# A decoder layer on one core: the down projection's products S4·R22 and S3·T3 one behind the other, T4 made a stage earlier, L22 and S3 kept divided

## The chip, the core and the metric

The kernel runs on one core of a Trainium2 chip. The metric is the device time of one execution in microseconds (us); the median of several runs counts. The engines are TensorE (PE in the rows; PEld is its weight load), VectorE (DVE), ScalarE (ACT), GpSimd (POOL) and SyncE (SP). SP and POOL issue transfers between DRAM and the on-chip memory; the rows write their queues as SPq and POOLq.

## The reference

One decoder layer over 1024 tokens of width 1024, in float32. The part that the change touches is the channel-mixing sub-layer at its end:

```
u = x * (1.0 + scale2) + shift2
h = jnp.square(jax.nn.relu(u @ w_up[l] + b_up[l]))        # 1024 x 4096
y = h @ w_down[l] + b_down[l]                             # 1024 x 1024
x = _layer_norm(DEEPNORM_ALPHA * x + (1.0 + gate2) * y, ln2_g[l], ln2_b[l])
```

Ahead of it stand the token-mixing sub-layer (a gated recurrence and a retention branch, merged by gates, and an output projection with a layer norm of its own) and the modulation vectors.

## The kernel before

**Precision.** Every float32 product is three fp32r products: `split` (L171 to L173) divides an operand into a high part (an ACT copy, L172) and a low part (a DVE subtraction, L173), and `mm3` (L177 to L179) adds high·high, high·low and low·high into one PSUM bank.

**Up projection.** `seven` makes the hidden rows in groups, each for 256 hidden rows j (16 of them) and all tokens, by seven products of quarter blocks; the first group is plain (`up_plain`). Its sums leave PSUM on DVE (L443). `use_square` applies the squared ReLU and makes, for each j, seven left operands of the down projection: L11, L12, L22 and the sums S1 to S4 of quarters of h (128 hidden rows by 512 tokens each). `keep_h` (L1488) writes each to DRAM (`h_d`, 256 KB) by POOL's queue.

**Down projection.** `down_seven` multiplies h by w_down, again with seven products of quarter blocks: left operands L and S by right operands R11, R21, R22 (quarters of w_down) and T1 to T4 (differences of them). Each product runs over 16 pairs j of hidden rows, 12 PE instructions (`multiply`) for a j, into four PSUM banks: set X (tags d, d, d, b) or set Y (a, a, c, c). The seven stand in four stages, and within a stage the two products alternate j by j:

```
stages = ((("L12", "R21", "Y", True), ("L11", "R11", "X", True)),
          (("S1", "T1", "Y", True), ("S2", "T2", "X", False)),
          (("S4", "R22", "Y", False), ("S3", "T3", "X", False)),
          (("L22", "T4", "X", False),))
```

For step n of this sequence `load(n)` brings the left operand from DRAM by SP's queue (tile hr, 4 buffers), and `prepare(n)` makes the right operand from the raw rows of w_down on DVE and splits both into one U tile (14 buffers of 8 KB, of which 4 hold T2 for all j). `prepare` runs five steps ahead of `multiply`, `load` three steps ahead of `prepare`. T4 = W21 - T2 is made in the third stage, over T2.

**Behind the products.** When a product's 16 pairs are done, its banks are copied (`keep`) or added (`add`, L1621) to the eight row blocks of the output in SBUF, row0 to row7, 128 tokens each. `first_part` (L1603, L1606, L1607: times the gate, plus the residual zp, statistics) runs on half a row block, `second_part` on a whole one: the aggregate (L1376), L1377, a power on POOL (L1378), then for each half L1613 and L1614 on DVE and the output transfer (L1615). Work put into the list `later` is taken one piece per step. In the last stage the last eight pairs (DOWN_TAIL) are multiplied row block by row block (tt = 0 to 3), each followed by its first and second part.

**What sets the order.** The order in which the code records the work, and a scheduler that interleaves it on each engine by when it could start; the order excerpts below are what it made.

Of the kernel before, what the change touches and what calls it, by code (L numbers as in the profile page):

```python
# [19 lines left out]
P = 128  # L20
# [23 lines left out]
DOWN_TAIL = 8  # L44
N_LARGE = 14

# [5 lines left out]

H_DEFER = 4


# [71 lines left out]
class Trunk:  # L127
# [1359 lines left out]
    def keep_h(self, j, name, t):  # L1487
        self.nc.gpsimd.dma_start(self.h_d[j][name], t)  # L1488

# [31 lines left out]
    def up_plain(self):  # L1521
        wt = [self.W(("up", 0, t)) for t in (0, 1)]
        places = iter("grrrgrg")
        tile = lambda: (self.tp.tile([P, 512], F32, tag="relu", bufs=4, name=self.uid("relu")) if next(places) == "r" else
                        self.wp.tile([P, 512], F32, tag="gate", bufs=2, name=self.uid("relu")))
        use = self.use_square(0, tile, (1, 1))
        for half in (0, 1):
            for m in (0, 1):
                use(m, half, self.dense_T(*wt[m], half), True)
                if (half, m) == (0, 0):  # L1530
                    yield


    def down_seven(self):
# [6 lines left out]
                  (("S1", "T1", "Y", True), ("S2", "T2", "X", False)),  # L1541
                  (("S4", "R22", "Y", False), ("S3", "T3", "X", False)),
                  (("L22", "T4", "X", False),))
        seq = [(s, j, p) for s, st in enumerate(stages) for j in range(J) for p in range(len(st))]
        t2 = [self.ut(F32) for _ in range(J // 4)]
        T2 = [t2[j // 4][:, j % 4] for j in range(J)]
        loaded, parts, raws = {}, {}, {}

        def load(n):
            s, j, p = seq[n]  # L1550
            t = loaded[n] = self.hp.tile([P, 512], F32, tag="hr", bufs=4, name=self.uid("hr"))
            nc.sync.dma_start(t, self.h_d[j][stages[s][p][0]])

        def prepare(n):
            s, j, p = seq[n]
            left, right = stages[s][p][:2]
            if n + 3 < len(seq) and n + 3 not in loaded:
                load(n + 3)
            if p == 0 and s < 3:
                raws[j] = self.W(("dn", s, j))  # L1560
            r = raws.get(j)
            tmp = lambda: self.hp.tile([P, 512], F32, tag="tf", bufs=2, name=self.uid("tf"))
            if right == "R21":
                src = r[0][:, 1]
            elif right == "R11":
                src = r[0][:, 0]
            elif right == "T1":
                src = self.t1 = tmp()
                V.tensor_tensor(src, r[0][:, 512:], r[0][:, :512], op=ALU.subtract)
            elif right == "T2":  # L1570
                src = T2[j]
                V.tensor_tensor(src, r[1], self.t1, op=ALU.subtract)
            elif right == "R22":
                src = r[0][:, 1]
            elif right == "T3":
                src = tmp()
                V.tensor_tensor(src, r[0][:, 1], r[0][:, 0], op=ALU.subtract)
                V.tensor_tensor(T2[j], r[1], T2[j], op=ALU.subtract)
            else:
                src = T2[j]  # L1580
            u = self.ut()
            self.split(u[:, 0], u[:, 1], loaded.pop(n))
            self.split(u[:, 2], u[:, 3], src)
            parts[n] = u

# [46 lines left out]
        for n, (s, j, p) in enumerate(seq):  # L1632
# [5 lines left out]
            if later:  # L1638
                later.pop(0)()
            if s == 3 and j >= J - DOWN_TAIL:  # L1640
                if j == J - 1:
# [9 lines left out]
            for tt in range(4):  # L1651
# [6 lines left out]
                elif (s, p) == (1, 0):  # L1658
                    keep(Y, 4 + tt, up)
                elif (s, p) == (1, 1):  # L1660
                    keep(X, tt, up)
                elif (s, p) == (2, 0):
                    add(Y, tt, up)
                    later.append(lambda tt=tt: first_part(tt, up))
                elif (s, p) == (2, 1):
                    add(X, 4 + tt, up)
                    later.append(lambda tt=tt: first_part(4 + tt, up))
            if (s, p) == (2, 1):
                later += [lambda tt=tt: second_part(tt) for tt in range(4)]


def build(ctx, tc, ins, out):
# [13 lines left out]
    k.ga_d, k.gb_d, k.y1_d = dt("ga_d", KT), dt("gb_d", KT), dt("y1_d", KT)  # L1686
    k.h_d = [{c: k.dp.tile([P, 512], F32, name=f"h_d{j}{c}") for c in ("L11", "L12", "L22", "S1", "S2", "S3", "S4")}
             for j in range(FT // 2)]
# [49 lines left out]
    two = lambda j, cs: wd[256 * j:256 * j + 256, cs].rearrange("(k p) c -> p k c", p=P)  # L1738
    for st in range(3):
        for j in range(FT // 2):  # L1740
            pcs = {0: [two(j, lo)],
                   1: [wd[256 * j:256 * j + P, :], wd[256 * j + P:256 * j + 256, up]],
                   2: [two(j, up), wd[256 * j + P:256 * j + 256, lo]]}[st]
            rest.append((pcs, [(("dn", st, j), "raw", None)]))
# [103 lines left out]
    with ExitStack() as sh:  # L1848
# [12 lines left out]
        with ExitStack() as se:  # L1861
            k.ev = k.pool("ev2", "left", se)
            k.e_bufs = 14
            up = k.seven(ups)
            next(up)
# [36 lines left out]
```

## Time and profile before

| | us |
|---|---|
| median of 3 runs | 2258.92 |
| lowest, highest run | 2257.53, 2260.2 |
| the profiled execution | 2258.29 |
| its span (first to last instruction) | 2256.5 |

The profiled execution lies 0.63 us below the median, and its span ends 1.79 us below its own time. The mean granted TensorE clock is 0.997 of full speed. The times in all rows are those of the profiled execution. A row's "idle before" is the time in which the engine stood still ahead of the instruction, and the name behind the arrow is what ended it.

### The profile page before, as it was taken

Reading aid. Unit: us, or ns where it says so; the run is one execution under the profiler, and the core shown is the slowest. Engines: PE = TensorE matmul, PEld = TensorE weight load, DVE = VectorE, ACT = ScalarE, POOL = GpSimd, SP = SyncE. Lnnn points to the kernel's source line nnn. Section 1 sums busy time; section 2 is a strip of 40 time slices with the busy share of each in tenths; the row PEclk is TensorE's granted clock in tenths of the full one; section 3 lists DMA queues with packets and bytes.
Section 4 is the critical chain, followed back from the end, with each engine's and each line's share of the span. In section 5 each row is a group of like instructions: output and inputs, shape, how many; then the busy total and the mean of one; then the engine's idle time right before and its main releaser. Section 6 shows DMA issues by size and latency. Waiting matters only on the chain. (4 is left out here: it accounts for less than half of the span.)

```text
span 2256.5 us, 29106 instructions
## 1 busy us (share of the span) xinstructions
PE 2215.7 (98%) x10214; PEld 1822.1 (81%) x10214; DVE 1660.4 (74%) x3024; ACT 967.3 (43%) x1625; POOL 282.1 (13%) x444
## 2 busy tenths in 40 slices
PE   6999999999999999999999999999999999999997
PEld 4888887888888888888877777888878888888886
DVE  7757777667878678889765556977796665577669
ACT  3533334433333333332354434443575555553441
POOL 0110111111111101010112221112112112100001
PEclk9999999999999999999999999999999999999999
DMA  9554644544343522113176667655344444787653
GB/s 309 183 167 161 208 136 164 169 135 140 135 141 117 172 89 75 57 66 104 60 254 201 209 204 258 211 163 179 112 150 156 152 154 151 265 289 247 215 164 131
DMA packets 229075, 375.33 MB, mean 166 GB/s; under 512 B 17096, under 2 KB 127424, under 8 KB 228672
## 3 DMA queue, kind: packets, MB, share of 16 engines
q1 hardware_dynamic: 200176, 279.66, 38.4%
q0 software_dynamic: 28432, 93.35, 11.2%
q8 instruction: 80, 1.31, 0.2%
q14 instruction: 67, 0.55, 0.1%
q10 hardware_dynamic: 320, 0.45, 0.1%
HBM read 275.87 MB, written 97.53 MB: 165 GB/s over the span
## 5 line engine op out<-in xcount | busy, mean ns | idle before, releaser
L177 PE MATMUL psd<-U,bh 128*128 128x512 f32 x616 | 241.9, 393 | 1.8 <-DVE e L443 1.8
L178 PE MATMUL psd<-U,bh 128*128 128x512 f32 x616 | 239.8, 389 | 0.0
L179 PE MATMUL psd<-U,bl 128*128 128x512 f32 x616 | 239.8, 389 | 0.0
L172 ACT ACTIVATE bh<-s 128x512 fp32r<-128x512 f32 x204 | 128.6, 631 | 239.7 <-PE psd L178 78.9
L178 PE MATMUL psd<-U,wh 128*128 128x512 f32 x504 | 199.6, 396 | 3.6 <-DVE U L173 3.3
L177 PE MATMUL psd<-U,wh 128*128 128x512 f32 x504 | 202.4, 405 | 0.4 <-ACT U L172 0.4
L179 PE MATMUL psd<-U,wl 128*128 128x512 f32 x504 | 201.8, 400 | 0.0
L172 ACT ACTIVATE bh<-raw 128x512 fp32r<-128x512 f32 x153 | 97.1, 638 | 206.1 <-PE psd L178 100.4
L173 DVE TENSOR_TENSOR bl<-raw,bh 128x512 fp32r<-128x512 f32 x153 | 104.5, 689 | 105.8 <-ACT bh L172 92.9
L173 DVE TENSOR_TENSOR bl<-s,bh 128x512 fp32r<-128x512 f32 x204 | 139.5, 685 | 49.4 <-ACT bh L172 49.3
L177 PEld LDWEIGHTS psd<-U,bh 128*128 128x128 f32 x616 | 115.6, 188 | 31.0 <-issue 3.5
L172 ACT ACTIVATE U<-hr 128x512 fp32r<-128x512 f32 x112 | 70.5, 630 | 151.0 <-issue 56.7
L179 PEld LDWEIGHTS psd<-U,bl 128*128 128x128 f32 x616 | 115.7, 188 | 24.2
L178 PEld LDWEIGHTS psd<-U,bh 128*128 128x128 f32 x616 | 115.7, 188 | 23.5
L172 ACT ACTIVATE wh<-raw 128x512 fp32r<-128x512 f32 (+1 forms) x78 | 52.7, 695 | 173.8 <-PE psd L178 136.2
L177 PE MATMUL psa<-U,bh 128*128 128x512 f32 x312 | 121.4, 389 | 0.0
L178 PE MATMUL psa<-U,bh 128*128 128x512 f32 x312 | 121.4, 389 | 0.0
L179 PE MATMUL psa<-U,bl 128*128 128x512 f32 x312 | 121.4, 389 | 0.0
L178 PEld LDWEIGHTS psd<-U,wh 128*128 128x128 f32 x504 | 95.5, 190 | 25.3 <-DVE U L173 7.3
L177 PEld LDWEIGHTS psd<-U,wh 128*128 128x128 f32 x504 | 95.1, 190 | 19.1 <-ACT U L172 2.3
L179 PEld LDWEIGHTS psd<-U,wl 128*128 128x128 f32 x504 | 95.3, 189 | 18.7
L173 DVE TENSOR_TENSOR U<-hr,U 128x512 fp32r<-128x512 f32 x112 | 76.7, 685 | 44.7 <-ACT U L172 44.5
(446 smaller groups left out, 5630.7 us busy)
## 6 DMA issues: line engine op xcount, KB each, us to landing
raw<-in_w_in SPq DMA_DIRECT2D x126, 512.0 KB
raw<-in_w_down SPq DMA_DIRECT2D x48, 512.0 KB
raw<-in_w_pb SPq DMA_DIRECT2D x36, 512.0 KB
adw<-in_w_ada SPq DMA_DIRECT2D x64, 256.0 KB
raw<-in_w_up SPq DMA_DIRECT2D x32, 512.0 KB
adw<-in_w_ada SPq DMA_DIRECT2D x16, 512.0 KB
rv_d<-e POOLq DMA_DIRECT2D x32, 256.0 KB, 3.8
rg_d<-e POOLq DMA_DIRECT2D x32, 256.0 KB, 2.4
```

Of the source, the lines that this page charges most:

```text
L172: pin(self.nc.scalar.activation(hi, src, AF.Copy))
L173: pin(self.nc.vector.tensor_tensor(lo, src, hi.bitcast(F32), op=ALU.subtract))
L177: r = mm(out, wh, uh, start=start, stop=False, skip_group_check=more)
L178: mm(out, wh, ul, start=False, stop=False, skip_group_check=more)
L179: return r, mm(out, wl, uh, start=False, stop=stop, skip_group_check=more)
```

## The change

The third stage becomes two: all 16 pairs of S4·R22 into Y, then all 16 of S3·T3 into X; L22·T4 follows as before. T4 is computed in the second stage behind the split of T2, from the lower rows of w_down that are there for T2; so the second stage loads these rows whole, and the new third stage loads the quarter W22 once more. The work of row blocks 0 to 3 is put into `later` behind S4·R22 and that of rows 4 to 7 behind S3·T3. L22 and S3 are split in the up projection, by `keep_h`, into two tiles (tag parts; 4 buffers for the first group, 3 for the others) and written as two fp32r tensors; the down projection loads the two straight into a U tile by POOL's queue, and takes that tile at `load`, not at `prepare`. U has 15 buffers instead of 14, and the program is built with a scratch of 4096 bytes for dynamic transfers where the default stood.

In the excerpts and the diff lines of the change stand two (helpers) or some twenty (`down_seven`) further down: L175 is L173, L399 is L397, L445 is L443, L1516, L1520, L1522, L1527 are L1506, L1510, L1512, L1517, L1594 is L1577, L1623, L1626, L1627, L1633, L1634, L1641 are L1603, L1606, L1607, L1613, L1614, L1621, and L1378, L1379 are L1376, L1377.

```diff
 DOWN_TAIL = 8
-N_LARGE = 14
+N_LARGE = 15
...
 H_DEFER = 4
+
+H_PARTS = ("L22", "S3")
...
     def keep_h(self, j, name, t):
-        self.nc.gpsimd.dma_start(self.h_d[j][name], t)
+
+        d = self.h_d[j][name]
+        if name not in H_PARTS:
+            self.nc.gpsimd.dma_start(d, t)
+            return
+        parts = [self.h_tile(F32R) for _ in d]
+        self.split(*parts, t)
+        for a, b in zip(d, parts):
+            self.nc.gpsimd.dma_start(a, b)
...
         stages = ((("L12", "R21", "Y", True), ("L11", "R11", "X", True)),
                   (("S1", "T1", "Y", True), ("S2", "T2", "X", False)),
-                  (("S4", "R22", "Y", False), ("S3", "T3", "X", False)),
-                  (("L22", "T4", "X", False),))
+                  (("S4", "R22", "Y", False),), (("S3", "T3", "X", False),), (("L22", "T4", "X", False),))
         seq = [(s, j, p) for s, st in enumerate(stages) for j in range(J) for p in range(len(st))]
+        last = len(stages) - 1
         t2 = [self.ut(F32) for _ in range(J // 4)]
         T2 = [t2[j // 4][:, j % 4] for j in range(J)]
         loaded, parts, raws = {}, {}, {}
 
         def load(n):
             s, j, p = seq[n]
+            d = self.h_d[j][stages[s][p][0]]
+            if isinstance(d, list):
+                u = loaded[n] = self.ut()
+                for e in (0, 1):
+                    nc.gpsimd.dma_start(u[:, e], d[e])
+                return
             t = loaded[n] = self.hp.tile([P, 512], F32, tag="hr", bufs=4, name=self.uid("hr"))
-            nc.sync.dma_start(t, self.h_d[j][stages[s][p][0]])
+            nc.sync.dma_start(t, d)
 
         def prepare(n):
             s, j, p = seq[n]
             left, right = stages[s][p][:2]
             if n + 3 < len(seq) and n + 3 not in loaded:
                 load(n + 3)
...
-            if p == 0 and s < 3:
+            if p == 0 and s < last:
...
             elif right == "T2":
                 src = T2[j]
-                V.tensor_tensor(src, r[1], self.t1, op=ALU.subtract)
+                V.tensor_tensor(src, r[1][:, 512:], self.t1, op=ALU.subtract)
             elif right == "R22":
-                src = r[0][:, 1]
+                src = r[0]
             elif right == "T3":
                 src = tmp()
                 V.tensor_tensor(src, r[0][:, 1], r[0][:, 0], op=ALU.subtract)
-                V.tensor_tensor(T2[j], r[1], T2[j], op=ALU.subtract)
             else:
                 src = T2[j]
-            u = self.ut()
-            self.split(u[:, 0], u[:, 1], loaded.pop(n))
+            u = loaded.pop(n)
+            if stages[s][p][0] not in H_PARTS:
+                hr, u = u, self.ut()
+                self.split(u[:, 0], u[:, 1], hr)
             self.split(u[:, 2], u[:, 3], src)
+            if right == "T2":
+                V.tensor_tensor(src, r[1][:, :512], src, op=ALU.subtract)
             parts[n] = u
...
-            if s == 3 and j >= J - DOWN_TAIL:
+            if s == last and j >= J - DOWN_TAIL:
...
                 elif (s, p) == (2, 0):
                     add(Y, tt, up)
                     later.append(lambda tt=tt: first_part(tt, up))
-                elif (s, p) == (2, 1):
+                elif (s, p) == (3, 0):
                     add(X, 4 + tt, up)
                     later.append(lambda tt=tt: first_part(4 + tt, up))
-            if (s, p) == (2, 1):
+            if (s, p) == (2, 0):
                 later += [lambda tt=tt: second_part(tt) for tt in range(4)]
...
-    k.h_d = [{c: k.dp.tile([P, 512], F32, name=f"h_d{j}{c}") for c in ("L11", "L12", "L22", "S1", "S2", "S3", "S4")}
+    k.h_d = [{c: [k.dp.tile([P, 512], F32R, name=f"h_d{j}{c}{e}") for e in "hl"] if c in H_PARTS else
+              k.dp.tile([P, 512], F32, name=f"h_d{j}{c}") for c in ("L11", "L12", "L22", "S1", "S2", "S3", "S4")}
...
-    for st in range(3):
+    for st in range(4):
         for j in range(FT // 2):
             pcs = {0: [two(j, lo)],
-                   1: [wd[256 * j:256 * j + P, :], wd[256 * j + P:256 * j + 256, up]],
-                   2: [two(j, up), wd[256 * j + P:256 * j + 256, lo]]}[st]
+                   1: [wd[256 * j:256 * j + P, :], wd[256 * j + P:256 * j + 256, :]],
+                   2: [wd[256 * j + P:256 * j + 256, up]],
+                   3: [two(j, up)]}[st]
...
         with ExitStack() as se:
             k.ev = k.pool("ev2", "left", se)
             k.e_bufs = 14
+            k.h_tile = lambda dt: k.ev.tile([P, 512], dt, tag="parts", bufs=3, name=k.uid("hp"))
```

**DVE behind the sums on Y.** Of the kernel before, the end of the old third stage (row_16792 to row_16795 are row blocks 0 to 3, row_16796 to row_16799 are 4 to 7):

```order
L1621 TENSOR_TENSOR row_16792<-row_16792,psa_16780 128x512
L1621 TENSOR_TENSOR row_16793<-row_16793,psa_16781 128x512
L1621 TENSOR_TENSOR row_16794<-row_16794,psc_16782 128x512
L1621 TENSOR_TENSOR row_16795<-row_16795,psc_16783 128x512
L1603 TENSOR_TENSOR row_16792<-row_16792,g_3251_16931 128x512
L1621 TENSOR_TENSOR row_16796<-row_16796,psd_16784 128x512
L1606 TENSOR_TENSOR row_16792<-row_16792,zp_18945 128x512
L1621 TENSOR_TENSOR row_16797<-row_16797,psd_16785 128x512
L1607 BN_STATS stats<-row_16792 128x6
L1621 TENSOR_TENSOR row_16798<-row_16798,psd_16786 128x512
L1621 TENSOR_TENSOR row_16799<-row_16799,psb_16787 128x512
L1603 TENSOR_TENSOR row_16793<-row_16793,g_3251_16931 128x512
```

Of the change, the end of S4·R22 (row_16984 to row_16987 are row blocks 0 to 3):

```order
L175 TENSOR_TENSOR U_18827<-tf_18910,U_18827 128x512
L1641 TENSOR_TENSOR row_16984<-row_16984,psa_16972 128x512
L1641 TENSOR_TENSOR row_16985<-row_16985,psa_16973 128x512
L1641 TENSOR_TENSOR row_16986<-row_16986,psc_16974 128x512
L1641 TENSOR_TENSOR row_16987<-row_16987,psc_16975 128x512
L1623 TENSOR_TENSOR row_16984<-row_16984,g_3315_17123 128x512
L1623 TENSOR_TENSOR row_16985<-row_16985,g_3315_17123 128x512
L1626 TENSOR_TENSOR row_16984<-row_16984,zp_18811 128x512
L1626 TENSOR_TENSOR row_16985<-row_16985,zp_18837 128x512
L1627 BN_STATS stats<-row_16984 128x6
L1627 BN_STATS stats<-row_16985 128x6
```

The sums on X (psd, psb) no longer stand between the sums on Y and the first parts of rows 0 to 3; in the change they come 52 rows further down.

**DVE at the end of the tail.** Before (row_16798 and row_16799 are row blocks 6 and 7, psb the last bank):

```order
L1607 BN_STATS stats<-row_16798 128x6
L1603 TENSOR_TENSOR row_16799<-psb_16787,g_3251_16931 128x512
L1376 BN_AGGR stats<-stats 128x2
L1606 TENSOR_TENSOR row_16799<-row_16799,zp_19342 128x512
L1377 TENSOR_SCALAR stats<-stats 128x1
L1613 SCALAR_TENSOR_TENSOR row_16798<-row_16798,stats,lg_16933 128x512 x2
L1614 SCALAR_TENSOR_TENSOR row_16798<-row_16798,stats,lb_16935 128x512 x2
L1607 BN_STATS stats<-row_16799 128x6
L1376 BN_AGGR stats<-stats 128x2
L1377 TENSOR_SCALAR stats<-stats 128x1
L1613 SCALAR_TENSOR_TENSOR row_16799<-row_16799,stats,lg_16933 128x512 x2
L1614 SCALAR_TENSOR_TENSOR row_16799<-row_16799,stats,lb_16935 128x512 x2
```

In the change (row_16991 is row block 7), the last seven rows:

```order
L1623 TENSOR_TENSOR row_16991<-psb_16979,g_3315_17123 128x512
L1626 TENSOR_TENSOR row_16991<-row_16991,zp_19470 128x512
L1627 BN_STATS stats<-row_16991 128x6
L1378 BN_AGGR stats<-stats 128x2
L1379 TENSOR_SCALAR stats<-stats 128x1
L1633 SCALAR_TENSOR_TENSOR row_16991<-row_16991,stats,lg_17125 128x512 x2
L1634 SCALAR_TENSOR_TENSOR row_16991<-row_16991,stats,lb_17127 128x512 x2
```

Before, the second part of row block 6 stands between the first part's operations of row block 7; in the change each row block's work stands in one piece.

**DVE at the start of the up projection** (relu and e are quarters of h, U of 128x1024 operands of the next products, bl a weight's low part, hp the tiles of the new split, L397 a sum for the operands). Before:

```order
L397 TENSOR_TENSOR U_13896<-U_13897,U_13896 128x1024
L173 TENSOR_TENSOR bl_14325<-s_14326,bh_14324 128x512
L173 TENSOR_TENSOR bl_14344<-s_14345,bh_14343 128x512
L1510 TENSOR_TENSOR relu_14240<-relu_14240,relu_14271 128x512
L397 TENSOR_TENSOR U_13896<-U_13897,U_13896 128x1024
L1512 TENSOR_TENSOR relu_14275<-relu_14240,relu_14139 128x512
L173 TENSOR_TENSOR bl_14374<-raw_14302,bh_14373 128x512
L1517 TENSOR_TENSOR relu_14280<-relu_14211,relu_14275 128x512
L397 TENSOR_TENSOR U_13897<-U_13897,U_13518 128x1024 x2
L173 TENSOR_TENSOR bl_14426<-raw_14013,bh_14425 128x512
L173 TENSOR_TENSOR U_14396<-U_13897,U_14395 128x1024
```

In the change:

```order
L175 TENSOR_TENSOR hp_14278<-relu_14275,hp_14277 128x512
L225 TENSOR_TENSOR s_14387<-raw_14043 128x512
L175 TENSOR_TENSOR bl_14367<-s_14368,bh_14366 128x512
L399 TENSOR_TENSOR U_13928<-U_13929,U_13928 128x1024
L175 TENSOR_TENSOR bl_14386<-s_14387,bh_14385 128x512
L1520 TENSOR_TENSOR relu_14272<-relu_14272,relu_14308 128x512
L175 TENSOR_TENSOR hp_14312<-relu_14308,hp_14311 128x512
L1522 TENSOR_TENSOR relu_14317<-relu_14272,relu_14171 128x512
L175 TENSOR_TENSOR bl_14416<-raw_14344,bh_14415 128x512
L1527 TENSOR_TENSOR relu_14322<-relu_14243,relu_14317 128x512
L399 TENSOR_TENSOR U_13928<-U_13929,U_13928 128x1024
L399 TENSOR_TENSOR U_13929<-U_13929,U_13550 128x1024 x2
```

The two hp rows are new; one stands ahead of the first sum for U, the other ahead of the second.

## Rows read from the trace of the kernel before

**Rows 1.** The page's first part: for each engine its busy time in us, its share of the span and its instructions.

```profile
PE 2215.7 (98%) x10214; PEld 1822.1 (81%) x10214; DVE 1660.4 (74%) x3024; ACT 967.3 (43%) x1625; POOL 282.1 (13%) x444
```

**Rows 2.** The waits of PE over the whole run: tile and line of the waiting product, what it waited for, us in total, times, longest.

```profile
PE psd L178 <- DVE U L173: 3.3, 6, 0.8
...
PE psd L177 <- DVE e L443: 2.4, 4, 0.7
```

**Rows 3.** The same for 1700 to 2257 us alone (its only row).

```profile
PE psd L177 <- DVE e L443: 0.5, 1, 0.5
```

**Rows 4.** Stretches by the stages of the down projection (the first, the second, the old third and the last): from:to, length, then busy us (and instructions) of PE, PEld, DVE, ACT, POOL; granted clock, share of the DMA engines, GB/s.

```profile
1938.00:2026.00 88.00, 87.45 (x387) 72.10 (x386) 57.26 (x92) 42.16 (x76) 2.70 (x5) 1.00 0.86 293
2026.00:2113.00 87.00, 87.00 (x385) 72.07 (x384) 64.01 (x103) 37.88 (x67) 0.00 (x0) 1.00 0.68 228
2113.00:2200.00 87.00, 87.00 (x385) 72.08 (x384) 58.59 (x95) 39.53 (x70) 0.00 (x0) 1.00 0.58 184
2200.00:2243.50 43.50, 43.50 (x192) 35.68 (x191) 43.47 (x82) 5.88 (x10) 5.88 (x6) 1.00 0.38 133
```

**Rows 5.** PE's last product, same columns.

```profile
2243.12 0.39 PE L179 MATMUL psb<-U 128*128 128x512 f32 x1
```

**Rows 6.** DVE's operations at the end: start us, us (of all, where x2 stands for two behind each other), engine, line, operation, out<-in, count.

```profile
2245.58 0.67 DVE L1603 TENSOR_TENSOR row<-psb,g 128x512 f32<-128x512 f32 x1
...
2246.96 1.40 DVE L1613 SCALAR_TENSOR_TENSOR row<-row,stats,lg 128x512 f32<-128x512 f32 x2
2248.28 1.41 DVE L1614 SCALAR_TENSOR_TENSOR row<-row,stats,lb 128x512 f32<-128x512 f32 x2
2249.61 0.69 DVE L1607 BATCH_NORM_STATS2 stats<-row 128x6 f32<-128x512 f32 x1
2250.32 0.21 DVE L1376 BATCH_NORM_AGGREGATE stats<-stats 128x2 f32<-128x12 f32 x1
2250.57 0.15 DVE L1377 TENSOR_SCALAR stats<-stats 128x1 f32<-128x1 f32 x1
2250.64 1.40 DVE L1613 SCALAR_TENSOR_TENSOR row<-row,stats,lg 128x512 f32<-128x512 f32 x2
2251.96 1.41 DVE L1614 SCALAR_TENSOR_TENSOR row<-row,stats,lb 128x512 f32<-128x512 f32 x2
```

**Rows 7.** DVE from the end of the old third stage to the tail's first row block, the first rows, two of the splits and the last ones.

```profile
2195.73 1.28 DVE L1621 TENSOR_TENSOR row<-row,psa 128x512 f32<-128x512 f32 x2
...
2198.12 0.68 DVE L1603 TENSOR_TENSOR row<-row,g 128x512 f32<-128x512 f32 x1
...
2231.07 0.68 DVE L173 TENSOR_TENSOR U<-U,U 128x512 fp32r<-128x512 f32 x1
...
2232.64 0.75 DVE L1613 SCALAR_TENSOR_TENSOR row<-row,stats,lg 128x512 f32<-128x512 f32 x1
...
2234.62 1.28 DVE L1603 TENSOR_TENSOR row<-psd,g 128x512 f32<-128x512 f32 x2
```

**Rows 8.** Starts behind one another, in the up projection: a product of PE, and DVE's operations behind it.

```profile
1913.16 0.39 PE L179 MATMUL psa<-U,bl 128*128 128x512 f32 x1
...
1913.64 0.69 DVE L443 TENSOR_TENSOR e<-psa,e 128x512 f32<-128x512 f32 x1 [1.65 <-PE psa L179]
...
1918.54 0.69 DVE L1510 TENSOR_TENSOR e<-e,e 128x512 f32<-128x512 f32 x1 [0.86 <-ACT e L1499]
1919.27 0.69 DVE L1512 TENSOR_TENSOR e<-e,e 128x512 f32<-128x512 f32 x1
```

**Rows 9.** POOL's last operation, same columns, and in brackets what its start waited for.

```profile
2250.80 0.99 POOL L1378 TENSOR_TENSOR stats<-stats,small 128x1 f32<-128x1 f32 x1 [2.70 <-DVE stats L1377]
```

**Rows 10.** Four stretches, columns as in rows 4: the start of the up projection, 200 us of its middle, a stretch of the gated part with the DMA engines full, and the first 50 us of the first stage of the down projection.

```profile
1639.80:1680.00 40.20, 39.43 (x172) 31.85 (x171) 40.16 (x55) 28.64 (x45) 5.95 (x11) 1.00 0.33 111
1700.00:1900.00 200.00, 200.00 (x884) 165.65 (x883) 127.13 (x191) 116.07 (x190) 38.61 (x72) 1.00 0.44 151
...
1370.00:1380.00 10.00, 8.66 (x36) 5.10 (x35) 6.01 (x11) 5.27 (x7) 3.02 (x5) 1.00 1.03 366
...
1950.00:2000.00 50.00, 50.00 (x222) 41.40 (x221) 26.94 (x43) 22.41 (x40) 0.00 (x0) 1.00 0.85 292
```

**Rows 11.** Two groups of the page's fifth part: line, engine, operation, tiles, count | busy us, mean ns of one | idle before, and what ended it.

```profile
L172 ACT ACTIVATE U<-hr 128x512 fp32r<-128x512 f32 x112 | 70.5, 630 | 151.0 <-issue 56.7
...
L173 DVE TENSOR_TENSOR U<-hr,U 128x512 fp32r<-128x512 f32 x112 | 76.7, 685 | 44.7 <-ACT U L172 44.5
```

**Rows 12.** A wait of PE in 1500 to 1700 us.

```profile
PE psd L178 <- DVE U L173: 0.7, 1, 0.7
```

**Rows 13.** One group of the page's list of DMA issues: count, KB each, median us from issue to landing.

```profile
h_d12L<-e POOLq DMA_DIRECT2D x3, 256.0 KB, 2.5
```

**Rows 14.** DVE's last sum of the up projection and PE's product behind it.

```profile
1943.27 0.68 DVE L443 TENSOR_TENSOR e<-psd,e 128x512 f32<-128x512 f32 x1
...
1944.01 0.50 PE L177 MATMUL psd<-U 128*128 128x512 f32 x1 [0.55 <-DVE e L443]
```

**Rows 15.** Issues of POOL's queue in line L1488: shortest, median, longest in ns, first and last start in us; and one of them in the timeline, which followed another at once.

```profile
L1488 POOL DMA_DIRECT2D h_d0S<-relu x4: 540/540/542, 1649.4 to 1657.2; - x4
...
1654.23 0.54 POOL L1488 DMA_DIRECT2D h_d0S<-relu  x1 [0.18 <-issue]
```

**Rows 16.** The waits of PE in 1000 to 1350 us.

```profile
PE psd L178 <- DVE U L173: 1.8, 3, 0.8
```

More of the change, by code (lines that the diff above doesn't have):

```diff
@@ L1525, in up_plain @@
                         self.wp.tile([P, 512], F32, tag="gate", bufs=2, name=self.uid("relu")))
+        self.h_tile = lambda dt: self.tp.tile([P, 512], dt, tag="parts", bufs=4, name=self.uid("hp"))
         use = self.use_square(0, tile, (1, 1))
@@ L1878 @@
     from concourse.bass_utils import run_bass_kernel_spmd
-    nc = bacc.Bacc("TRN2", target_bir_lowering=False, num_devices=1)
+    nc = bacc.Bacc("TRN2", target_bir_lowering=False, num_devices=1, dynamic_dma_scratch_size=4096)
     arrays, aps = {}, {}
```

## The prediction

> **What bounds the kernel now.** The page's first part says that TensorE is busy 98% of the span and VectorE 74% [rows 1]: a change can win only where PE stands still, or behind PE's last product. The list of waits of PE comes next. Over the whole run PE waits 3.3 us for a split's lower half (U, L173) and 2.4 us for a sum of the up projection (e, L443) [rows 2]; from 1700 us on it waits once, 0.5 us [rows 3]. The table by stages of the down projection shows PE at 87.00 of 87 us in the second and the third, and at 43.50 of 43.5 us in the last [rows 4]. So within the down projection nothing is to be had but that 0.5 us. In the last stage VectorE is busy 43.47 of 43.50 us: it is late there, and its rows show by how much. PE's last product starts at 2243.12 and lasts 0.39, so it ends at 2243.51 [rows 5]. DVE takes that bank only at 2245.58, and between then and 2253.37 it still does the products of the row block before (L1613, L1614 at 2246.96 to 2249.69) [rows 6]. The span of 2256.5 us ends 3.13 us behind DVE's last operation: the last output transfer, which this change leaves alone.
>
> **Why DVE is late there.** From 2195.73 to 2234.62 it does, interleaved: eight sums (L1621, the first four in one piece), the first parts of eight row blocks (three operations each), some fourteen splits, and the second parts of rows 0 to 3 (for one, 2232.64 to 2234.62 is its last) [rows 7]. The first row block of the tail was ready in PSUM at about 2200 + 8 x 2.72 + 5.44 = 2227.2 (PE spends 43.5/16 = 2.72 us on a pair of hidden rows, and 8 x 2.72/4 = 5.44 on a row block of the tail); DVE took it at 2234.62, 7.4 us late.
>
> **Part 1, the stage split in two.** The products, their count and their banks are the same, so PE's 130.5 us of the last two stages stay. What moves is DVE's work: the four sums on Y and the first and second parts of rows 0 to 3 become due at 2156.5 instead of 2200, in a stage where DVE has 87 - 58.59 = 28 us free [rows 4]. Four sums (0.60 each, by the spacing of 2195.73 to 2198.12 [rows 7]), twelve first operations (0.60 each), four second parts (0.2 + 0.1 + 2.65 each, by 2250.32 to 2253.37 [rows 6]) are 2.4 + 7.2 + 11.8 = 21.4 us. With part 3 the last stage also loses some seven splits of L22, 4.2 us. It keeps four sums, twelve first operations and four splits of T4 (the other twelve stand ahead of the sums in the new order): 2.4 + 7.2 + 2.4 = 12 us in the 27 us before 2227.2, so DVE is on time at the tail. Of the banks: the four sums on X must be read before L22 adds to them. A bank is done 2.04, 1.36, 0.68 and 0 us before 2200 and wanted again 2.72 us later; sums of 0.60 each that start at 2198.6 (behind the last split ahead of them, whose buffer PE frees at 2197.3) end 0.7 us early. No stall is counted.
>
> Then each row block of the tail costs DVE a chain of its own: sum-product L1603, +0.73 L1606, +0.73 L1607 (a dependent operation starts 0.73 behind, 1918.54 to 1919.27 [rows 8]), +0.71 the aggregate, +0.25 L1377, +0.07 L1613 (2 x 0.66), L1614 (1.41) [rows 6]. That is 0.73 + 0.73 + 0.71 + 0.25 + 0.07 + 1.32 + 1.41 = 5.22 us, below PE's 5.44 for a row block, so DVE waits for PE at each. The last one starts 0.09 us behind PE (PE's 1913.16 + 0.39, DVE at 1913.64 [rows 8]), at 2243.60, and ends at 2248.82. POOL's power operation (0.99 us, starting 0.23 behind L1377 [rows 9]) ends at 2247.24, before L1614 needs it at 2247.41. Before, the end is 2253.37. **The gain is 4.55 us**, and 0 if DVE stayed late; it cannot be more, since PE's end does not move.
>
> **Part 2, T4 made in stage 1.** One DVE operation per pair moves from the third stage to the second, where DVE has 23 us free [rows 4]; 16 x 0.60 = 9.6. It makes 4 MB more traffic of weights. Stage 1 needs 1.5 MB per 5.44 us, 289 GB/s (decimal), where 228 flow now; the first stage moved 293 with the engines' share at 0.86, and one stretch 366 at 1.03 [rows 4, 10]. I take nothing for it; the cover is the raw buffers' lead.
>
> **Part 3, L22 and S3 kept divided.** 32 splits, each an ACT copy (0.63) and a DVE subtraction (0.685 alone, 0.60 in a row) [rows 11], move into the up projection. There DVE is busy 127.13 of 200 us, ACT 116.07, and PE 200.00 [rows 10]; two more operations of each per 19 us are covered. Where it is not covered is the start of the up projection, 1639.8 to 1680: DVE is busy all the time there and PE 39.43 of 40.2 us [rows 10], with one wait of 0.7 us for a split [rows 12]. Four of the new splits fall in this stretch, 4 x 0.60 = 2.4 us if all were on the path; if a buffer must wait for a transfer to land (2.5 us [rows 13]) up to 0.6 more. Nothing, if they fall behind the operands PE needs next. In the new order two of them stand some ten operations ahead of the split of a 128x1024 operand of the next products, which so comes 1.2 us later; thirteen products (0.227 each, 43.5/192 [rows 4], 3 us) have moved ahead of the ones that need it. The other two come with h1, ahead of a weight's split (bl), with little cover. I take 0.4 us, near the lower end, and keep 0 to 3.0. At the seam (1943.27, PE waits 0.55 [rows 14]) the order of DVE changes around the same operation; it can vanish or double: 0 taken.
>
> POOL's queue gets 32 more writes in the up projection and 64 loads in the last two stages, two per 2.72 us. An issue takes 0.54 us, also while DVE is full (the first h_d0S at 1649.4 [rows 10, 15]); with 0.18 between, two are 1.44 of 2.72 us. Behind the loads on POOL stand only the power operations of rows 0 to 3, which nobody but DVE's second parts waits for. The trap named in the Trainium skill (SBUF — State Buffer, section "SBUF: two separate sides") speaks against this: a transfer from POOL's queue issued while DVE runs a two-port fast-mode operation cannot have its descriptors written; its next section ("A bandwidth-pool intuition that's wrong") has 0.62 us becoming some 3.1. By it two loads would take 6.2 of 2.72 us. The row's 0.54 beside a full DVE (subtractions) speaks against it here, and the sum goes by the row.
>
> **Part 4, the 15th U buffer and the smaller scratch.** A buffer lets earlier loads in the retention part start a little sooner. There PE waits 1.8 us for splits [rows 2, 16]. Between -1.5 and +1.5 us; 0 taken.
>
> **Sum.** The profiled execution took 2258.29 us, 0.63 below the median 2258.92. 2258.29 - 4.55 + 0.4 = 2254.14 for it, 2254.77 on the median. I say 2254.7.
>
> **Rivals.**
> A, the forecast: 2253.7 to 2255.6 (gain 3.3 to 5.2 with the unknowns at part 3 and 4).
> B, the buffer helps: the 1.8 us of retention waits and the seam's 0.5 go too: 4.55 + 1.8 + 0.5 = 6.9 us at most, 2252.0. For it: the waits are there; against it: a split waits there for a transfer from DRAM whose start depends on more than a U buffer.
> C, the full stretch takes the gain back: DVE is saturated, the four splits land on PE's path with 1.8 to 3.0 us: 2256.1 to 2257.4. For it: DVE busy all 40 us. Against: products put ahead.
> D, slower: the new loads don't keep up. Stage S3·T3 needs 1 MB per 2.72 us, 385 GB/s, and no 10 us row is above 366 at a share of 1.03 [rows 10]. At plain copies' rate of 292/0.85 = 343 GB/s it needs 16 x 1.05 MB/343 = 49 us for 43.5: 5.5 us behind, which the lead of eight pairs (21.8 us, since loads are issued eight ahead) hides. If a transfer into the fp32r type costs c times a plain one, both stages take (8.4 + 16.8 c) MB at 343 GB/s, and this passes 87 + 21.8 us at c = 1.72. At c = 2 it is 122.5 us, 13.7 late: 2254.7 + 13.7 = 2268. It shows as slower from c = 1.9 on (9 us late). For it: no row of before shows such a transfer. The Trainium skill (DMA: Bandwidth & Descriptors, section "SWDGE vs HWDGE vs iDMA") says a copy into float32r always counts as a cast and goes by the software queue alone; it gives no rate, and no run here shows one yet. Against: a transfer moves the same bytes.
> E, slower by POOL: an issue that had to wait for the end of a DVE operation (up to 0.69 us [rows 11]) would be 0.54 + 0.18 + 0.69 = 1.41, two of them 2.82 per 2.72 us: 32 x 0.10 = 3.2 us late, hidden by the lead. It hurts only from 1.7 us an issue; at 2 us it would be (4.0 - 2.72) x 32 = 41, less 21.8, 19 us: 2274. By the Trainium skill's 3.1 us (SBUF — State Buffer, the section on the wrong bandwidth-pool intuition) the estimate is (6.2 - 2.72) x 32 - 21.8 = 90 us, 2344.
> F, no effect: DVE stays late for another cause (second parts that wait for POOL behind a load), gain under 1: 2258 to 2259.
>
> **Numbers.** Chances: A 0.55, B 0.18, C 0.14, D 0.08, E 0.02, F 0.03. A measurement of this kernel can tell 0.2% (4.5 us) from no change, so faster is below 2254.40, slower above 2263.4. The forecast stands at that line: of A, 0.24 lies below it. Faster 0.24 + 0.18 = 0.42; slower 0.08 + 0.02 = 0.10; the rest, 0.31 + 0.14 + 0.03 = 0.48, is the same. The range 2251.8 to 2258.5 takes in A, B, C, and leaves out D, E and F, 0.13.
>
> **What would show it.** Right: DVE's L1603 on the last bank starts 0.1 us behind PE's end, DVE's last operation ends 5.3 us behind it, PE stays at 43.5 of 43.5 us in the last stages, and the DVE share of the last stage falls to some 65%. Wrong at C: more PE waits in 1640 to 1680. Wrong at D or E: PE waits for DMA U, or POOL's issues longer than 0.54. Wrong at F: DVE takes the last bank late, or rows 0 to 3 are finished behind 2200. Wrong at B: waits for splits near 1150 to 1172 gone.

## The result: slower by 0.33%, and where the profile after shows it

The changed kernel takes 2265.1 us (median of 7, 2262.86 to 2267.87) against 2258.1 for the kernel before (7, 2256.36 to 2260.2): ratio 1.0033, 95% interval 1.0024 to 1.0043, some 7 us slower. The profiled execution took 2263.87 us (before 2258.29), with a span of 2262.1 (2256.5).

The tail did what was forecast. DVE at the end (columns as in [rows 6]):

```profile
2253.11 0.69 DVE L1623 TENSOR_TENSOR row<-psb,g 128x512 f32<-128x512 f32 x1 [0.22 <-PE psb L181]
...
2256.93 1.41 DVE L1634 SCALAR_TENSOR_TENSOR row<-row,stats,lb 128x512 f32<-128x512 f32 x2
```

PE's last product (answers to [rows 5]):

```profile
2252.69 0.39 PE L181 MATMUL psb<-U 128*128 128x512 f32 x1
```

PE ends at 2253.08, DVE takes the last bank 0.03 behind that and ends at 2258.34, 5.26 us behind PE. Before, that was 2253.37 - 2243.51 = 9.86: 4.60 us won here. But PE's end itself came 9.57 us later. Where PE lost these is seen from its idle time in four stretches, each a row's length less its PE time. Before:

```profile
0.00:700.00 700.00, 679.09 (x2996) 553.92 (x2997) 515.96 (x972) 277.25 (x462) 80.42 (x149) 1.00 0.52 169
700.00:1635.00 935.00, 929.45 (x4547) 766.94 (x4547) 701.64 (x1358) 374.27 (x629) 132.75 (x174) 1.00 0.45 150
1635.00:1700.00 65.00, 64.23 (x281) 52.20 (x280) 58.66 (x81) 46.65 (x77) 12.47 (x23) 1.00 0.46 157
1700.00:2238.00 538.00, 537.45 (x2372) 444.85 (x2371) 368.83 (x584) 269.13 (x459) 52.53 (x94) 1.00 0.57 194
```

After:

```profile
0.00:700.00 700.00, 680.39 (x3001) 554.43 (x3002) 516.58 (x974) 278.08 (x464) 80.45 (x149) 1.00 0.52 169
700.00:1635.00 935.00, 929.80 (x4551) 767.89 (x4550) 700.92 (x1358) 375.71 (x634) 134.65 (x176) 1.00 0.45 150
1635.00:1700.00 65.00, 62.46 (x272) 50.34 (x271) 60.96 (x87) 48.16 (x78) 14.51 (x27) 1.00 0.54 176
1700.00:2238.00 538.00, 531.49 (x2330) 439.06 (x2329) 360.12 (x573) 264.46 (x452) 100.59 (x185) 0.99 0.70 230
```

PE's idle time goes from 20.91, 5.55, 0.77 and 0.55 us to 19.61, 5.20, 2.54 and 6.51. So nothing was lost ahead of the up projection (1.65 us less there); 1.8 us were lost at its start, and 6.0 us behind 1700. These last are two waits (answers to [rows 3], where there was one of 0.5):

```profile
PE psd L179 <- DVE e L445: 3.7, 1, 3.7
PE psd L179 <- DVE row L1641: 2.8, 1, 2.8
```

The first stands at the seam of up and down projection. PE's rows there:

```profile
1942.94 0.39 PE L180 MATMUL psa<-U 128*128 128x512 f32 x1
1947.04 0.50 PE L179 MATMUL psd<-U 128*128 128x512 f32 x1 [3.71 <-DVE e L445]
```

PE needs the third psd bank from about 1943.3 on. DVE's rows tell why it doesn't get it:

```profile
1941.78 0.68 DVE L445 TENSOR_TENSOR e<-psd,e 128x512 f32<-128x512 f32 x1
...
1943.92 0.69 DVE L1520 TENSOR_TENSOR e<-e,e 128x512 f32<-128x512 f32 x1 [0.25 <-ACT e L1509]
1945.09 0.69 DVE L175 TENSOR_TENSOR hp<-e,hp 128x512 fp32r<-128x512 f32 x1 [0.48 <-DMA h_d15S3h<-hp]
1945.70 0.68 DVE L1522 TENSOR_TENSOR e<-e,e 128x512 f32<-128x512 f32 x1
1946.31 0.68 DVE L445 TENSOR_TENSOR e<-psd,e 128x512 f32<-128x512 f32 x1
```

L445 at 1946.31 frees the bank. It came at 1943.27 before [rows 14]. Ahead of it in DVE's order stand the new split of the last group (hp, 1945.09), which waited 0.48 for the write of another hp tile to land (three buffers), and L1520, which came 2.46 us later than its counterpart before (1941.46). L1520 stands behind splits of left operands; how much of its delay comes from their transfers is not shown, since such splits waited for transfers before the change too.

The second wait stands behind the first stage of the down projection. DVE, SP and PE there:

```profile
2029.45 0.69 DVE L1603 TENSOR_TENSOR U<-raw,U 128x512 f32<-128x512 f32 x1
...
2031.38 0.69 DVE L1586 TENSOR_TENSOR tf<-raw 128x512 f32<-128x512 f32 x1
2034.96 0.69 DVE L1589 TENSOR_TENSOR U<-raw,tf 128x512 f32<-128x512 f32 x1 [2.88 <-DMA raw<-in_w_down]
2035.57 1.88 DVE L1641 TENSOR_TENSOR row<-row,psd 128x512 f32<-128x512 f32 x3
```

```profile
2030.17 0.33 SPq L317 DMA_DIRECT2D raw<-in_w_down  x1
```

```profile
2033.12 0.39 PE L181 MATMUL psc<-U 128*128 128x512 f32 x1
2036.30 0.64 PE L179 MATMUL psd<-U 128*128 128x512 f32 x1 [2.79 <-DVE row L1641]
```

The four sums on X (L1641), which free the banks that PE wants from 2033.5 on, stand behind T2 (L1589), which waited 2.88 us for raw rows of w_down. Their load was issued at 2030.17, 0.03 behind the end of T4 (L1603, 2029.45 + 0.69): T4 is the last to read a raw buffer, so it decides when the next load starts. (The trace names only the tensor. That this load is the one T2 waited for follows from a count: by then DVE had done seven T2 and five T4, so two of the four raw buffers held rows that still waited for their T4, a third held those of the T1 at 2031.38 (L1586), and the fourth was the one just freed. T4 is late in this way since the code puts it behind the split of T2, which takes a U tile of its own.)

Each wait cost more than its length. The clock behind the two (columns as in [rows 4], the third last is the granted clock):

```profile
1942.00:1943.30 1.30, 1.30 (x6) 0.75 (x4) 1.30 (x3) 0.87 (x3) 0.00 (x0) 1.00 1.12 392
1943.30:1947.00 3.70, 0.03 (x1) 0.00 (x0) 2.96 (x6) 1.94 (x4) 1.45 (x3) 1.00 0.99 312
1948.00:1950.00 2.00, 2.00 (x6) 1.55 (x5) 1.01 (x3) 1.71 (x3) 0.00 (x0) 0.50 1.14 358
...
2038.00:2039.50 1.50, 1.50 (x5) 1.19 (x4) 1.50 (x4) 0.00 (x0) 0.00 (x0) 0.50 0.00 0
```

It falls from 1.00 to 0.50 (2.4 to 1.2 GHz) behind the wait. The 13 products from 1947.04 take 4.68 us to 1951.72 instead of 13 x 0.227 = 2.95, the ten from 2036.30 take 3.98 instead of 2.27: 1.7 us lost each time.

The account closes: PE's idle time in the four stretches grew by 6.1 us, and half clock cost 3.4; 9.5 of the 9.57 us by which PE ended later. Less 4.60 at the tail, and 0.63 more for the last transfer (3.76 instead of 3.13 us behind DVE's end), is 5.6, the growth of the span.

### The profile page after: what moved, and what is told of

It is laid out like the page before. It is cut to its first block, busy times and chain, and to the rows that moved or that the text cites. A ratio compares the mean times of both kernels' runs of the same rounds, so it can differ in the third digit from the quotient of the medians.

```text
span 2262.1 us, 29266 instructions
## 1 busy us (share of the span) xinstructions
PE 2219.2 (98%) x10214; PEld 1823.9 (81%) x10214; DVE 1657.8 (73%) x3024; ACT 966.4 (43%) x1625; POOL 334.2 (15%) x540
## 5 line engine op out<-in xcount | busy, mean ns | idle before, releaser
L175 DVE TENSOR_TENSOR bl<-s,bh 128x512 fp32r<-128x512 f32 x204 | 139.6, 685 | 46.9 <-ACT bh L174 46.6
L175 DVE TENSOR_TENSOR bl<-raw,bh 128x512 fp32r<-128x512 f32 x153 | 104.4, 689 | 94.4 <-ACT bh L174 79.3
L174 ACT ACTIVATE U<-hr 128x512 fp32r<-128x512 f32 x80 | 50.3, 629 | 104.8 <-PE psc L181 23.2
L175 DVE TENSOR_TENSOR U<-hr,U 128x512 fp32r<-128x512 f32 x80 | 54.8, 687 | 43.2 <-ACT U L174 42.9
```

What stands on the lines that cost most here:

```text
L174: pin(self.nc.scalar.activation(hi, src, AF.Copy))
L175: pin(self.nc.vector.tensor_tensor(lo, src, hi.bitcast(F32), op=ALU.subtract))
```

## The experiments

The theory after this reading (W): the two waits and the start of the up projection are the price of T4's place and of the divided operands, and the split of the stage by itself wins the tail. Rivals: more traffic makes everything late (L); the 15th U buffer and the scratch spoil the order upstream (U). All times below are medians of 11 runs, each with the kernel before on the same chip. The views show one execution of each kernel, and that one can lie well off the median: 2.5 us above it in e1_no_parts (the slowest of its eleven), 2.6 below it in e3_both, 3.3 below it in f2_parts_mid.

**e1_no_parts.** No operand kept divided.

```diff
-H_PARTS = ("L22", "S3")
+H_PARTS = ()
```

> The changed kernel without its kept-divided operands: L22 and S3 are written once and split in the down projection, as before. Theory W (two waits): in the changed kernel PE stood 3.71 us at the seam of up and down projection (1947.04, behind DVE's last sum L445, which stands behind the new hp splits of j = 15), with some 1.7 us more at half clock behind it, where before it stood 0.55; and 1.66 us in 1650 to 1700 where before it stood 0.04. Both go, the 2.79 us at the change of stages (2036.30) stays: 2265.1 - 4.9 - 1.6 = 2258.6 us. Rival L (more transfers make everything late): hr and raw transfers come late because of 4 MB more weights, of which this run takes away nothing, so the seam's wait stays above 2 us: 2262 to 2264. Rival U (the 15th U buffer and the small scratch spoil the order upstream): no change, 2264 to 2265.

Measured: 2262.75 us, ratio 1.0013 (1.0004 to 1.0022). PE's waits behind 1700:

```profile
PE psd L179 <- DVE row L1641: 4.7, 1, 4.7
PE psd L179 <- DVE e L445: 1.2, 1, 1.2
```

The seam's wait fell from 3.7 to 1.2 us and PE's idle time in 1635 to 1700 from 2.54 to 0.85, as W said. The wait at the change of stages did not stay at 2.8 but grew to 4.7, again with half clock behind it, so the time fell by 3 us (from 7.0 to 3.9 above the kernel before) where 6.5 were expected. Rival L wanted more than 2 us at the seam and rival U no change; neither fits. The divided operands are a cause of the first two waits. That the third grew was not expected. DVE there:

```profile
2036.09 0.69 DVE L1589 TENSOR_TENSOR U<-raw,tf 128x512 f32<-128x512 f32 x1 [1.79 <-DMA raw<-in_w_down]
2036.70 1.87 DVE L1641 TENSOR_TENSOR row<-row,psd 128x512 f32<-128x512 f32 x3
```

PE came to this place 0.75 us earlier than in the changed kernel and the sums 1.13 us later (2036.70 for 2035.57), again behind a T2 that waits for raw rows; together that is the 1.9 us. Why the raw rows came later was not followed.

**e2_t4_in_s4.** T4 made in the stage of S4·R22.

```diff
-                V.tensor_tensor(src, r[1][:, 512:], self.t1, op=ALU.subtract)
+                V.tensor_tensor(src, r[1], self.t1, op=ALU.subtract)
...
-                src = r[0]
+                src = r[0][:, 512:]
...
-            if right == "T2":
-                V.tensor_tensor(src, r[1][:, :512], src, op=ALU.subtract)
+            if right == "R22":
+                V.tensor_tensor(T2[j], r[0][:, :512], T2[j], op=ALU.subtract)
...
-                   1: [wd[256 * j:256 * j + P, :], wd[256 * j + P:256 * j + 256, :]],
-                   2: [wd[256 * j + P:256 * j + 256, up]],
+                   1: [wd[256 * j:256 * j + P, :], wd[256 * j + P:256 * j + 256, up]],
+                   2: [wd[256 * j + P:256 * j + 256, :]],
```

> T4 is made in the stage of S4·R22 (the lower rows of w_down loaded whole there) instead of in the stage of S1 and S2; all else as changed. The bytes in all are the same. Theory W: the 2.79 us wait at 2036.30 comes from DVE's T2, which waits for raw rows whose buffer was held longer by T4, with the sums on X queued behind it; it goes, with 1.8 us at half clock behind it: 2265.1 - 4.6 = 2260.5 us. Rival L: the same bytes move, the wait moves to the next stage or stays: 2264 to 2266. Rival U: no change.

Measured: 2262.48 us, ratio 1.0015 (1.0006 to 1.0023). The one wait behind 1700 is the seam's:

```profile
PE psd L179 <- DVE e L445: 3.5, 1, 3.5
```

The wait at the change of stages is gone with the same bytes moved in all, and did not move to the next stage, as L had it. But this edit takes both T4 and its bytes out of the second stage, so it does not part the two; f3b_raw5_14u does. The time is 2.0 us above W's forecast. The profiled execution lost 2.7 us in 700 to 1635 that the changed kernel didn't lose (7.87 of idle time for 5.20); over all these kernels that stretch lies between 5.2 and 7.9.

**e3_both.** The two edits together.

> Both at once: no kept-divided operands, and T4 made in the stage of S4·R22; what is left of the change is the split of the stage, the 15th U buffer and the small scratch. Theory W: 2265.1 - 4.9 - 1.6 - 4.6 = 2254.0 us, DVE on time in the tail (last operation 5.3 us behind PE's end) though 32 splits are back in the down projection. Rival U: 2257 or more, with PE's waits ahead of 1640 us larger than before. A third, D: the splits of S3 and L22 make DVE late in the tail again, 2256 to 2258.

Measured: 2256.11 us, ratio 0.9988 (0.9979 to 0.9997). One wait is left behind 1700, as before the change:

```profile
PE psd L179 <- DVE e L445: 0.6, 1, 0.6
```

The time is 2.1 us above W's forecast and within D's range, so the tail has to decide between them:

```profile
2242.89 0.39 PE L181 MATMUL psb<-U 128*128 128x512 f32 x1
...
2247.14 1.41 DVE L1634 SCALAR_TENSOR_TENSOR row<-row,stats,lb 128x512 f32<-128x512 f32 x2
```

DVE ends 2248.55 - 2243.28 = 5.27 us behind PE: it is on time, and D falls. Against the kernel before, the two edits together win 9.7 us, more than the sum of what each won alone (3.1 and 3.4); the longer third wait in e1_no_parts and the loss ahead of 1635 in e2_t4_in_s4 fit that.

**e4_before_15u.** The kernel before with the buffer and the scratch.

```diff
-N_LARGE = 14
+N_LARGE = 15
...
-    nc = bacc.Bacc("TRN2", target_bir_lowering=False, num_devices=1)
+    nc = bacc.Bacc("TRN2", target_bir_lowering=False, num_devices=1, dynamic_dma_scratch_size=4096)
```

> The kernel before with 15 U buffers and the scratch of 4096 bytes alone. Theory W: nothing happens in the down projection, 2258.1 with 1.5 us either way by the waits ahead of 1640 us. Rival U: these two are what spoils the changed kernel upstream, 2260 to 2263.

Measured: 2258.24 us, ratio 0.9995 (0.9986 to 1.0003): no difference. In the kernel before, the two do nothing, and U falls there.

**f1_split_14u.** e3_both with 14 buffers and the old scratch: only the split of the stage, and T4 in the stage of S4·R22. The edit against e3_both:

```diff
-N_LARGE = 15
+N_LARGE = 14
...
-    nc = bacc.Bacc("TRN2", target_bir_lowering=False, num_devices=1, dynamic_dma_scratch_size=4096)
+    nc = bacc.Bacc("TRN2", target_bir_lowering=False, num_devices=1)
```

> Only the split of the stage, with T4 made in the stage of S4·R22: no kept-divided operands, 14 U buffers and the scratch as before. Theory W (the tail's 4.55 us are real, everything else of the change costs): 2258.5 - 4.55 = 2254 us, give or take the 1.5 us by which the order upstream moves; DVE's last operation 5.3 us behind PE's end. Rival U (the 15th buffer is what brings DVE its lead): DVE late in the tail, 2256 to 2258.

Measured: 2254.76 us, ratio 0.9981 (0.9972 to 0.9989), 4.0 us faster than before, as W said, and the lowest median of all kernels here (its interval overlaps that of e3_both, so what the 15th buffer and the scratch do in this kernel is not told apart from nothing). Its waits behind 1635, and its tail (PE's last product and DVE's last operation):

```profile
PE psd L179 <- DVE e L445: 0.9, 1, 0.9
PE psd L180 <- DVE U L175: 0.8, 1, 0.8
```

```profile
2245.82 0.39 PE L181 MATMUL psb<-U 128*128 128x512 f32 x1
...
2250.06 1.41 DVE L1634 SCALAR_TENSOR_TENSOR row<-row,stats,lb 128x512 f32<-128x512 f32 x2
```

DVE ends 2251.47 - 2246.21 = 5.26 us behind PE. The tail's gain needs neither the divided operands nor the 15th buffer.

**f2_parts_mid.** e2_t4_in_s4 with L22 and S3 kept divided for j = 2 to 14 alone.

```diff
+def divided(j, name):
+    return name in H_PARTS and 2 <= j <= 14
...
-        if name not in H_PARTS:
+        if not divided(j, name):
...
-            if stages[s][p][0] not in H_PARTS:
+            if not divided(j, stages[s][p][0]):
...
-    k.h_d = [{c: [k.dp.tile([P, 512], F32R, name=f"h_d{j}{c}{e}") for e in "hl"] if c in H_PARTS else
+    k.h_d = [{c: [k.dp.tile([P, 512], F32R, name=f"h_d{j}{c}{e}") for e in "hl"] if divided(j, c) else
```

> T4 in the stage of S4·R22, and L22 and S3 kept divided for j = 2 to 14 alone; those of the first two groups and of the last are split in the down projection. Theory W: it is the hp splits of j = 15 that stand ahead of DVE's last sums at the seam (3.5 us of waiting in the run with T4 moved), and those of j = 0 and 1 that cost 1.6 us in 1640 to 1700; both waits go to about 0.6 and 0.9, and the time is that of the run without divided operands, 2255 to 2256.5. Rival L: the 26 more writes and the POOL loads themselves make hr and raw late: the seam's wait stays above 2 us, 2260 or more. If it is below 2254.5, keeping divided is worth something in the middle.

Measured: 2257.59 us, ratio 0.9991 (0.9982 to 1.0000). Waits behind 1635 (its lines stand four further down):

```profile
PE psd L183 <- DVE e L449: 1.7, 1, 1.7
PE psd L184 <- DVE U L179: 0.9, 1, 0.9
```

The time is outside both W's range (2255 to 2256.5) and L's (2260 or more). The start of the up projection is back at 0.9, so it was the operands of j = 0 and 1. The seam's wait halved, from 3.5 to 1.7: the divided operands of j = 15 were part of it, not all. The middle's divided operands win nothing that these runs can show.

**g1_parts_to_12.** The same for j = 2 to 12.

```diff
-    return name in H_PARTS and 2 <= j <= 14
+    return name in H_PARTS and 2 <= j <= 12
```

> As the run with parts kept for j = 2 to 14, but only for j = 2 to 12. At the seam 1.7 us of waiting were left there with no hp split of j = 15 on DVE; the writes of h_d14 landed 5.4 us behind their issue where they take 3.2 without divided operands. Theory S1 (the doubled writes of the last two groups collide with the down projection's first loads, and DVE's sums stand behind splits that wait for them): the wait at the seam falls to 0.6 to 0.9 us and the h_d14 writes land in some 3.2 us. Theory S2 (the order on DVE alone, set for the whole phase): the wait stays at 1.5 us or more.

Measured: 2255.91 us, ratio 0.9989 (0.9979 to 0.9998). The landing of the last writes but one, in f2_parts_mid and here (median us from issue to landing is the last number):

```profile
h_d14S<-e POOLq DMA_DIRECT2D x3, 256.0 KB, 5.4
```

```profile
h_d14S<-e POOLq DMA_DIRECT2D x4, 256.0 KB, 3.1
```

The wait at the seam:

```profile
PE psd L183 <- DVE e L449: 1.4, 1, 1.4
```

The writes of j = 14 land sooner (5.4 us to 3.1), but that is not what PE waited for: the wait went only from 1.7 to 1.4, between the two theories. Without any divided operand it is 0.56 to 1.2 (e3_both, f1_split_14u, e1_no_parts), with no edit near it. So some 0.6 us of it vary from kernel to kernel by themselves; that the order on DVE does this is likely and not shown, and the remainder stays open.

**f3b_raw5_14u.** The changed kernel with a fifth raw buffer.

```diff
-N_LARGE = 15
+N_LARGE = 14
...
-        t = self.wr.tile([P, 1024], F32, tag="raw", bufs=4, name=self.uid("raw"))
+        t = self.wr.tile([P, 1024], F32, tag="raw", bufs=5, name=self.uid("raw"))
```

(and the same number for the other two tiles of that tag)

> The changed kernel with T4 where the change puts it, but five raw buffers instead of four (and 14 U buffers, to make room). Theory W: the 2.79 us wait at the change of stages comes from raw buffers that T4 holds longer; a fifth takes most of it, under 1 us is left there, the seam's 3.7 us stay: 2265 - 3.5 = 2261.5 us. Rival L: the larger traffic of that stage is the cause: the wait stays at 2 to 5 us, 2264 to 2266.

Measured: 2259.51 us, ratio 1.0005 (0.9996 to 1.0014). Waits behind 1635:

```profile
PE psd L179 <- DVE e L445: 1.6, 1, 1.6
PE psd L179 <- ACT e L433: 0.8, 1, 0.8
PE psd L180 <- DVE U L175: 0.8, 1, 0.8
PE psc L179 <- ACT bh L174: 0.7, 1, 0.7
```

With T4 where the change puts it and the same bytes in the same stage, the wait at the change of stages is gone: what was missing was a free raw buffer, which T4 held, and the larger traffic by itself does not make the wait. (The run also has one U buffer less than the changed kernel; e2_t4_in_s4, with 15, lost the wait too.) The seam's wait fell as well, from 3.7 to 1.6, though the divided operands of j = 15 are all there. So they do not set its length alone, and what else does stays open. This is also why the time lies 2.0 us below W's forecast.

## Why the prediction was wrong, step by step

- **The tail** (part 1) was right, in mechanism and size: DVE's end was forecast 5.31 us behind PE's and is 5.26, the gain 4.55 us and is 4.60; VectorE is on time at every row block, and its share of the last stage fell to 60% (25.97 of 43.5 us), where some 65% were named. "PE's end does not move", which the prediction took for granted, is what failed: PE's end came 9.57 us later, by the steps that follow.
- **T4** (part 2) is the first step that failed. "I take nothing for it; the cover is the raw buffers' lead" compared rates (289 GB/s needed; 293 and, in one stretch, 366 moved elsewhere) and DVE's free time, and left out that the moved operation is the last reader of a raw buffer, and that DVE's queue holds the sums on PE's banks behind it. It cost 2.8 us of waiting and 1.7 at half clock. The prediction named what stands behind a waiting instruction for POOL's queue (part 3), and did not ask it for DVE's.
- **The seam** (part 3) was priced at 0 with a bound of 0.55 either way. It cost 3.2 us of waiting more than before and 1.7 at half clock. The new splits of the last group stand there on DVE in front of the last sums; the prediction looked for them only at the start of the up projection. That the divided operands are a cause is shown twice (3.7 to 1.2 in e1_no_parts, 3.5 to 0.6 between e2_t4_in_s4 and e3_both); f3b_raw5_14u shows that they are not the whole of it.
- **The start of the up projection** (part 3): 0.4 taken, 0 to 3.0 kept; PE's idle time in 1635 to 1700 grew by 1.8. Rival C's place was right, and so was its size (1.8 to 3.0), in part by luck: it named a full DVE, and of the waits there 1.4 us are for ACT, which carries the other half of each new split:

```profile
PE psd L179 <- ACT e L433: 0.8, 1, 0.8
PE psc L179 <- ACT bh L174: 0.6, 1, 0.6
```

- **The half clock** had no place in the sum: no wait of before behind 1635 is longer than 0.73 us.
- **The 15th buffer** (part 4, rival B): no difference in the kernel before (e4_before_15u).
- **Rivals D and E** fell, and F with the tail. From 2156.5 to 2209.6, which takes in the stage S3·T3 that asks for 385 GB/s (the last 43.5 us), PE is busy 53.10 of 53.1 us. This view answers to [rows 4] and [rows 10], and the two POOL issues to [rows 15]:

```profile
2180.00:2190.00 10.00, 10.00 (x46) 8.29 (x45) 10.00 (x21) 3.69 (x6) 6.62 (x10) 1.00 1.10 330
2156.50:2209.60 53.10, 53.10 (x236) 43.96 (x235) 40.83 (x73) 13.37 (x23) 27.39 (x49) 1.00 1.09 344
```

```profile
2182.13 0.54 POOL L1566 DMA_DIRECT2D U<-h_d15S3l  x1
2182.87 0.53 POOL L1566 DMA_DIRECT2D U<-h_d0L22h  x1 [0.20 <-issue]
```

With the fp32r transfers among them, 344 GB/s flow over 53.1 us at a share of 1.09. That is the 343 by which D counted plain copies, so c is near 1 and far from 1.72; the engines are full, and the lead hides what is missing to 385, as D's sum for c = 1 has it. An issue takes 0.53 to 0.54 us while DVE is busy 10.00 of 10 us. By the trap named in the Trainium skill (SBUF — State Buffer, section "SBUF: two separate sides") they would starve beside a fast-mode DVE operation; the trace shows no such wait beside the operations that DVE runs here (L1633, L1634, splits and subtractions), and whether one of these is in that mode no row shows.

For the profiled execution 2254.14 us were forecast and 2263.87 measured. The 9.7 us between them are the seam with 4.9, T4 with 4.5 and the start of the up projection with 1.4 more than was taken for it, 0.6 more for the last transfer, and 1.65 less ahead of 1635.

The range (2251.8 to 2258.5) missed since T4 was taken at nothing and the seam was bounded by a short wait of before, and no case had two of the places lost at once.

## What to carry to other kernels

When an operation is moved to where "the engine has time", ask of it three things apart from its length: which buffer it is the last to read, what it waits for, and which operations stand behind it in that engine's order; here a subtraction of 0.69 us cost 4.5. The places to look at are those where PE changes its PSUM banks, since in both of the long waits here PE stood there for DVE sums that came behind operations waiting for something else. And take a change apart before judging it: its first part alone was 4.0 us faster, the three others took 11 us away together.

## What was not expected of the hardware

Behind waits of PE of 2.79 and 3.71 us (the changed kernel), 3.48 (e2_t4_in_s4) and 4.67 (e1_no_parts) the granted clock stood at 0.50 for 3 to 5 us, with 1.7 us lost behind each of the first two; behind waits of 1.68 us (f2_parts_mid) and 1.58 (f3b_raw5_14u) it stayed at 1.00. So in this kernel, which is bound by PE, the wait of 2.79 us cost 4.5.
